# Gated DeltaNet stage of a decoder step: state scaling to GpSimd, first taps to ScalarE, masks by selection, z gates read from the PSUM bank

## The chip, the cores and the metric

The kernel runs on one NeuronCore of a Trainium2 chip. The metric is device time in microseconds for one call, the median of several runs. Five engines work side by side, each through its own instruction list in order: TensorE (PE, matmuls; PEld are its weight loads), VectorE (DVE), ScalarE (ACT), GpSimd (POOL) and SyncE (SP, which issues nearly all DMAs here). An instruction that waits holds up everything behind it on its engine.

## The reference, cut to what matters

One inference step of a decoder layer for 256 prompt tokens and 8 samples of 8 tokens each, 320 columns in all. One input projection feeds two branches: a gated DeltaNet (GDN) with 16 key heads and 32 value heads, and a sparse attention. The parts that the change touches:

```python
y = sum(xp[:, i:i + L] * w[i] for i in range(CONV_W)); silu(y)          # short convolution, 4 taps
decay = exp(where(incl, G[..., :, None] - G[..., None, :], -inf))        # causal mask on the gates
s = s * gt_c[..., None, None] + einsum('bhck,bhcv->bhkv', kt_c, u)       # matrix state, 128 x 128 per head and sample
y = rms_norm(o, gdn_norm_g) * silu(z)                                    # output norm, gated by z
```

## The kernel before, in words

All large projections are matmuls of 128 output channels by 320 columns. A weight block is streamed in two halves ("units") of 128 x 1024: SP loads it into `raw` (six halves in flight), ScalarE rounds it to `whi` (line 380), VectorE makes the remainder `wlo = raw - whi` (line 381), three buffers each, and TensorE does 24 matmuls per unit (`pm<-xh,whi`, `pm<-xl,whi`, `pm<-xh,wlo`, lines 403 to 410). This main stream runs from 205 us to the end; a unit is about 3.5 us of TensorE.

Everything else is side work: Python generators that emit a few instructions at a time between the units (`side_round`, line 305). What is emitted where is decided while the program is built, by a planner: the class `Clock` (lines 76 to 193) keeps a modelled time for each engine, a generator is resumed once the modelled TensorE time has reached the time that it last yielded, and `force` (line 329) emits side work at once when the main stream needs a buffer. So a price or a yield that is changed moves instructions on all engines, and on the chip each engine then runs its list in that fixed order.

The GDN stage lies at some 705 to 1660 us, in eight groups of two key heads (four value heads). For each group:

- `conv` (line 1761), 64 calls in the program: ScalarE copies a block to `xp`, VectorE does tap 0 as a TENSOR_SCALAR into a PSUM bank `u` and taps 1 to 3 as SCALAR_TENSOR_TENSOR, ScalarE the tanh (`cth`), VectorE the gate.
- `z_done` (line 1887), 28 calls, and `z_early` (line 1319), 4: ScalarE copies z with the norm's weight as scale, ScalarE does a tanh into a second tile, VectorE joins them, SP stores the result to DRAM (`d_z`). The tiles are the ring `zf` of four; `norm_gen` uses the same ring to load z again and store y (`d_ya`).
- `gb_gen` (line 1896), 16 calls: gates are loaded, VectorE adds a 128 x 384 mask `mask3` for two heads, ScalarE does six exponentials.
- `inverse` (line 2007), 8 calls: a 48 x 32 x 32 triangular inverse on GpSimd, 31 pairs of TENSOR_TENSOR (`tmpx`, `X`), then through DRAM (`d_x`): SP writes `X` and its transpose `blk`, reads 15 pieces back into `XT`, `X` and `blk`, and TensorE joins the blocks in four steps. All of this stands in SP's one queue together with the `raw` loads.
- `prompt_chain` and `sample_chain` (lines 2155 and 2232), 16 calls each: short matmuls with copies and scalings between them. At the end of `sample_chain` (lines 2279 to 2284) VectorE updates the state `S` (128 x 2048) with 16 SCALAR_TENSOR_TENSOR of 128 x 128, `S * gtr + ps`.
- `norm_gen` (line 2294), 16 calls: ScalarE squares `ot` six times into `sc`; VectorE, GpSimd (the power -0.5) and VectorE again make six factors; ScalarE scales `ot` with them, six instructions `ot<-ot,sc`, right behind whatever was emitted before.

In this trace every instruction shows the line of one helper (L64), so groups are told apart by tile names.

Of the kernel before, what the change touches and what calls it, by code (L numbers as in the profile page):

```python
# [17 lines left out]
NP = 256  # L18
# [57 lines left out]
class Clock:  # L76
# [54 lines left out]
    def cost(self, name, op, outs, ins):  # L131
        n = max(self.free(a) for a in outs[:1] + ins) if ins else self.free(outs[0])
        if name == "tensor":
            if op == "transpose":
                return 0.01 if ins[0].shape[0] == 32 else max(outs[0].shape[-1], 32) * 2 / 2400.0
            lhs, rhs = ins
            n = self.free(rhs)
            if lhs.dtype == F32R:
                return n * 1.1 / 2400.0
            if lhs.dtype == BF:  # L140
                return n / 2400.0
            k, m = lhs.shape[0], lhs.shape[1]
            part = 0.32 if m <= 32 else 0.62 if m <= 64 else 1.0
            part *= 0.29 if k == 32 and rhs.shape[1] == NB else 0.62 if k <= 64 else 1.0
            return max(n, 32) * 4 / 2400.0 * part + 0.01
        if name == "vector":
            fast = op in ("tensor_copy", "memset", "tensor_scalar")
            sb = all(a.space == outs[0].space for a in ins)
            return 0.16 + n * (0.0006 if fast and sb else 0.00106)
        if name == "scalar":  # L150
            return 0.19 + n * 0.00084 + 0.19 * (len(outs) > 1)
        if op == "memset":
            return 0.1 + n * 0.0009
        return 0.25 + n * (0.0018 if op == "tensor_copy" else 0.0028)
# [51 lines left out]
class Kernel:  # L206
# [1112 lines left out]
    def z_early(self, p, h):  # L1319
        self.force(lambda: len(self.t_r.free) >= 2)  # L1320
        z, t = self.t_r.get(), self.t_r.get()
        self.act(z, p[:, :NT], AF.Copy, scale=self.gh)
        self.act(t, p[:, :NT], AF.Tanh, scale=0.5)
        self.stt(z, t, 1.0, z, OP.add, OP.mult)
        self.t_r.put(t)
        self.store(self.d_z[h], z, self.t_r)
# [372 lines left out]
    def gdn_open(self):  # L1699
# [8 lines left out]
        self.mask3 = a.tile([128, 384], F32, name="mask3")  # L1708
# [19 lines left out]
        for c0, m0 in ((0, 0), (128, 0), (256, 128)):  # L1728
            nc.vector.tensor_copy(self.mask3[:, c0:c0 + 128], self.mask[:, m0:m0 + 128])
# [31 lines left out]
    def conv(self, p, cs, blk, dests, slot, then):  # L1761
# [11 lines left out]
        self.ts(u[:, 0:344], xp[:, 0:344], wv(0), None, OP.mult)  # L1773
# [113 lines left out]
    def z_done(self, p, h):  # L1887
        self.force(lambda: self.zf.free and self.cth.free)
        z, t = self.zf.get(), self.cth.get()
        self.act(z, p[:, :NT], AF.Copy, scale=self.gh)  # L1890
        self.act(t[:, :NT], p[:, :NT], AF.Tanh, scale=0.5)
        self.stt(z, t[:, :NT], 1.0, z, OP.add, OP.mult)
        self.cth.put(t)
        self.store(self.d_z[h], z, self.zf)

    def gb_gen(self, h):
# [7 lines left out]
        self.tt(gb, gb, self.mask3.rearrange("p (o i) -> p o i", o=1).to_broadcast([128, 2, 384]), OP.add)  # L1904
# [212 lines left out]
    @staticmethod  # L2117
    def scal(G, e):
        sst = G["sst"]
        s = lambda v, t: sst[:, 26 + 6 * e + 3 * v + t:27 + 6 * e + 3 * v + t]  # L2120
        stl = lambda v, t: sst[:, 38 + 6 * e + 3 * v + t:39 + 6 * e + 3 * v + t]
        return s, stl
# [32 lines left out]
    def prompt_chain(self, h, G):  # L2155
# [20 lines left out]
        for v in range(2):  # L2176
            self.ts(wt[:, v, :], p[:, 128 * v:128 * v + 128], stl(v, 0), None, OP.mult)
# [28 lines left out]
        for v in range(2):  # L2206
            self.ts(wt[:, v, :], p[:, 128 * v:128 * v + 128], stl(v, 1), None, OP.mult)
# [24 lines left out]
    def sample_chain(self, h, G):  # L2232
# [21 lines left out]
        self.R.put(R)  # L2254
        for v in range(2):
            self.stt(xr[:, v, :], p[:, 128 * v:128 * v + 128], self.neG[:, 2, hv + v:hv + v + 1], vt[:, 2, v, :],
                     OP.mult, OP.add)
# [11 lines left out]
        for v in range(2):  # L2269
            self.ts(wt[:, v, :], p[:, 128 * v:128 * v + 128], stl(v, 2), None, OP.mult)  # L2270
        self.ps_side.put(p)
        self.drop_T(G)
        yield
        yield from self.need(self.ps_side, 4)
# [19 lines left out]
    def norm_gen(self, h, G):  # L2294
# [294 lines left out]
```

## Time and profile before

| | |
|---|---|
| time, median of 3 runs | 2140.52 us (2138.27 to 2140.97) |
| profiled execution: its time, its span | 2134.91 us, 2133.2 us |
| TensorE busy | 2089.9 us, 98% |
| VectorE, ScalarE, GpSimd busy | 1419.2 us (67%), 968.4 us (45%), 464.1 us (22%) |
| mean share of the 16 DMA engines in use, in 50 us stretches of the GDN stage | 0.60 to 0.91 |

Rows of a waits view read: engine and tile, who ended the wait, total us, times, longest. Rows of a timeline: start, duration, engine, operation, tiles, and in brackets the idle time before it and who ended it. Rows of the grouped view: engine, operation, tiles, shape, count, busy us, mean ns of one, idle time before. Rows of a windows view: stretch and length, then busy us and count of PE, PEld, DVE, ACT and POOL, the granted TensorE clock, DMA share, GB/s.

### The profile page before, as it was taken

How to read it: one execution, taken by the hardware profiler on the slowest of the kernel's cores; microseconds unless marked ns; L12 is line 12 of the kernel's file. 1: busy time of each engine (PE TensorE's matmuls, PEld its weight loads, DVE VectorE, ACT ScalarE, POOL GpSimd, SP SyncE). 2: the span in 40 equal slices, each digit the busy share in tenths (PEclk: the TensorE clock that was granted, in tenths of full speed). 3: DMA queues.
4: the chain of work that ended last, by engine and by line, in shares of the span. 5: the costliest groups of instructions: out<-in, count | busy, mean ns of one | idle time of the engine just before them, and what ended most of it. 6: DMA issues, size and time to landing. Idle time of an engine off the chain costs nothing.

```text
span 2133.2 us, 45095 instructions
## 1 busy us (share of the span) xinstructions
PE 2089.9 (98%) x17741; PEld 2021.9 (95%) x17741; DVE 1419.2 (67%) x2858; ACT 968.4 (45%) x2202; POOL 464.1 (22%) x654
## 2 busy tenths in 40 slices
PE   7999999999999999989999999999999999999997
PEld 7999999999999999889999999999999999999997
DVE  4676658899845577857877787778665645445543
ACT  4225443333434455465646564656554534233343
POOL 1001000000010019441835082708080000000000
PEclk9999999999999999999999999999999999999999
DMA  9996658885696766766867686868687877555562
GB/s 346 333 337 183 189 155 258 242 256 146 190 282 191 222 174 177 192 179 180 229 176 209 173 231 166 221 169 244 163 242 213 250 208 212 167 155 146 166 179 83
DMA packets 714149, 439.04 MB, mean 206 GB/s; under 512 B 73968, under 2 KB 697296, under 8 KB 711632
## 3 DMA queue, kind: packets, MB, share of 16 engines
q1 hardware_dynamic: 709856, 413.50, 68.8%
q0 software_dynamic: 3616, 21.02, 2.8%
q8 instruction: 139, 2.28, 0.4%
q10 hardware_dynamic: 464, 1.65, 0.2%
q14 instruction: 74, 0.61, 0.1%
HBM read 386.81 MB, written 48.94 MB: 204 GB/s over the span
## 4 chain that ended last, share of the span: by engine, by line
PE 64%; issue 22%; DVE 5%; ACT 3%; DMA 3%; SPq 1%; POOL 1%; DVEq 0%; POOLq 0%; ACTq 0%
PE pm L64 49%; PE ps L64 14%; DVE S L64 2%; SPq L64 1%; DVE wlo L64 1%; DMA raw<-in_w_ada_dram 1%; ACT whi L64 1%; DVE ps L64 1%; ACT ot L64 1%; ACT ps L64 1%; DMA rawx<-in_w_ada_dram 1%; POOL X L64 0%; ACT vt L64 0%; POOL tmpx L64 0%; DVE w L64 0%
## 5 line engine op out<-in xcount | busy, mean ns | idle before, releaser
L64 PE MATMUL pm<-xh,whi 128*128 128x320 f32 (+1 forms) x3108 | 941.3, 317 | 10.4 <-ACT whi L64 9.1
L64 PE MATMUL pm<-xl,whi 128*128 128x320 f32 (+1 forms) x3108 | 911.8, 307 | 0.4 <-DVE xl L64 0.3
L64 DVE TENSOR_TENSOR wlo<-raw,whi 128x1024 fp32r<-128x1024 f32 x466 | 586.7, 1267 | 258.7 <-ACT whi L64 242.2
L64 PEld LDWEIGHTS pm<-xh,whi 128*128 128x128 f32 x3108 | 586.0, 189 | 33.6 <-issue 17.6
L64 PEld LDWEIGHTS pm<-xl,whi 128*128 128x128 f32 x3108 | 586.4, 189 | 1.5 <-DVE xl L64 0.8
L64 ACT ACTIVATE whi<-raw 128x1024 fp32r<-128x1024 f32 x466 | 489.7, 1059 | 176.7 <-PE pm L64 109.4
L64 PE MATMUL pm<-xh,wlo 128*128 128x320 f32 (+1 forms) x3108 | 522.7, 308 | 2.5 <-DVE wlo L64 2.4
L64 PEld LDWEIGHTS pm<-xh,wlo 128*128 128x128 f32 x3108 | 470.2, 188 | 3.8 <-DVE wlo L64 3.7
L64 POOL TENSOR_TENSOR X<-X,tmpx 48x31 f32<-48x31 f32 (+15 forms) x248 | 182.1, 734 | 19.4
L64 POOL TENSOR_TENSOR tmpx<-blk,X 48x31 f32<-48x31 f32 (+15 forms) x248 | 162.8, 656 | 105.6 <-DMA blk<-d_b 87.6
L64 DVE SCALAR_TENSOR_TENSOR ps<-xp,cs,ps 128x344 f32<-128x344 f32 x192 | 111.5, 581 | 6.8
L64 POOL TENSOR_TENSOR sc<-sc,mh 128x6 f32<-128x6 f32 (+1 forms) x24 | 41.7, 1736 | 297.9 <-DVE sc L64 261.4
L64 PE MATMUL pm<-y1h,whi 128*128 128x320 f32 x336 | 99.5, 309 | 1.3 <-ACT whi L64 0.9
L64 POOL TENSOR_TENSOR rfin<-rfin,mh 128x3 f32<-128x3 f32 x1 | 0.8, 848 | 455.0 <-DVE rfin L64 455.0
L64 PE MATMUL pm<-y1l,whi 128*128 128x320 f32 x336 | 99.2, 308 | 0.0
L64 ACT ACTIVATE xp<-pm 128x256 f32<-128x256 f32 (+1 forms) x128 | 31.9, 302 | 83.4 <-PE pm L64 83.4
L64 POOL DMA_INDIRECT a<-in_cache_k_dram,idx x8 | 7.5, 936 | 280.2 <-PE ps L64 265.3
L64 DVE SCALAR_TENSOR_TENSOR S<-S,gtr,ps 128x128 f32<-128x128 f32 x256 | 67.4, 341 | 0.3 <-PE ps L64 0.3
L64 PE MATMUL ps<-xh,whi 128*128 128x320 f32 (+1 forms) x220 | 64.7, 309 | 0.0
L64 PEld LDWEIGHTS pm<-y1h,whi 128*128 128x128 f32 x336 | 62.9, 187 | 1.8 <-ACT whi L64 1.8
L64 PE MATMUL ps<-xl,whi 128*128 128x320 f32 (+1 forms) x220 | 63.7, 304 | 0.0
L64 PEld LDWEIGHTS pm<-y1l,whi 128*128 128x128 f32 x336 | 63.0, 187 | 0.0
(415 smaller groups left out, 2774.5 us busy)
## 6 DMA issues: line engine op xcount, KB each, us to landing
raw<-in_w_in_dram SPq DMA_DIRECT2D x328, 512.0 KB
raw<-in_w_pa_dram SPq DMA_DIRECT2D x64, 512.0 KB
rawx<-in_w_ada_dram SPq DMA_DIRECT2D x18, 1024.0 KB
a<-in_w_ada_dram SPq DMA_DIRECT2D x16, 1024.0 KB
S<-in_state_gdn_dram SPq DMA_DIRECT2D x32, 512.0 KB
out_dram<-S SPq DMA_DIRECT2D x32, 512.0 KB
raw<-in_w_pb_dram SPq DMA_DIRECT2D x32, 512.0 KB
raw<-in_w_out_dram SPq DMA_DIRECT2D x32, 512.0 KB
```

The lines of the kernel that those rows point to most:

```text
L64: made = fn(*args, **kw)
```

## The change

- State: GpSimd scales `S` by the decay in one TENSOR_TENSOR of 128 x 2048 as soon as the matmuls that read the old state are emitted; VectorE then only adds, four TENSOR_TENSOR of 128 x 512, one per bank.
- Convolution: tap 0 goes to ScalarE (a Copy with scale, from `xp` into the bank).
- Masks: `mask3` is gone; GpSimd writes the mask value by five AFFINE_SELECT per head pair. The planner gets a price for that operation.
- z: one tanh into the tile, and VectorE reads the other factor from the PSUM bank; the norm's weight moves into the last product of `norm_gen`. The second tile is no longer needed.
- The two scalings of `wt` per step become one TENSOR_TENSOR over both heads.
- `norm_gen`: one VectorE instruction fewer, the EPS added by GpSimd, and a new yield 1.5 us of modelled time behind the factors before the six ScalarE scalings are emitted. `sample_chain` yields until `S` is scaled before the last matmuls are emitted.

```diff
             return 0.19 + n * 0.00084 + 0.19 * (len(outs) > 1)
-        if op == "memset":
-            return 0.1 + n * 0.0009
+        if op in ("memset", "affine_select"):
+            return (0.1 if op == "memset" else 0.3) + n * 0.0009
         return 0.25 + n * (0.0018 if op == "tensor_copy" else 0.0028)
...
-        self.mask3 = a.tile([128, 384], F32, name="mask3")
...
         wv = lambda t: cs[:, blk, 24 + t:25 + t]
-        self.ts(u[:, 0:344], xp[:, 0:344], wv(0), None, OP.mult)
+        self.act(u[:, 0:344], xp[:, 0:344], AF.Copy, scale=wv(0))
         for t in range(1, 4):
...
     def z_done(self, p, h):
-        self.force(lambda: self.zf.free and self.cth.free)
-        z, t = self.zf.get(), self.cth.get()
-        self.act(z, p[:, :NT], AF.Copy, scale=self.gh)
-        self.act(t[:, :NT], p[:, :NT], AF.Tanh, scale=0.5)
-        self.stt(z, t[:, :NT], 1.0, z, OP.add, OP.mult)
-        self.cth.put(t)
+        self.force(lambda: self.zf.free)
+        z = self.zf.get()
+        self.act(z, p[:, :NT], AF.Tanh, scale=0.5)
+        self.stt(z, z, 1.0, p[:, :NT], OP.add, OP.mult)
         self.store(self.d_z[h], z, self.zf)
...
         yield
-        self.tt(gb, gb, self.mask3.rearrange("p (o i) -> p o i", o=1).to_broadcast([128, 2, 384]), OP.add)
+        self.emitted += 1
+        g = gb[:, :, 0:256].rearrange("p v (t i) -> p v t i", t=2)
+        nc.gpsimd.affine_select(g, g, pattern=[[0, 2], [0, 2], [1, 128]], compare_op=OP.is_ge, fill=NEG, base=0,
+                                channel_multiplier=-1)
+        for v in range(2):
+            g = gb[:, v, 256:384].rearrange("p (b q) -> p b q", b=8)
+            nc.gpsimd.affine_select(g, g, pattern=[[-16, 8], [0, 16]], compare_op=OP.is_ge, fill=NEG, base=0,
+                                    channel_multiplier=1)
+            g = gb[:, v, 256:384].rearrange("p (b q t) -> p b q t", b=8, q=2)
+            nc.gpsimd.affine_select(g, g, pattern=[[16, 8], [0, 2], [1, 8]], compare_op=OP.is_ge, fill=NEG, base=0,
+                                    channel_multiplier=-1)
         yield
...
         s = lambda v, t: sst[:, 26 + 6 * e + 3 * v + t:27 + 6 * e + 3 * v + t]
-        stl = lambda v, t: sst[:, 38 + 6 * e + 3 * v + t:39 + 6 * e + 3 * v + t]
+        stl = lambda t: sst[:, 38 + 6 * e + t:38 + 6 * e + 4 + t:3].rearrange("p (v o) -> p v o", o=1).to_broadcast([128, 2, 128])
         return s, stl
...
             self.act(wf[:, v, :], p[:, 128 * v:128 * v + 128], AF.Copy, scale=s(v, 0))
-        for v in range(2):
-            self.ts(wt[:, v, :], p[:, 128 * v:128 * v + 128], stl(v, 0), None, OP.mult)
+        self.tt(wt, p[:, 0:256].rearrange("p (v d) -> p v d", v=2), stl(0), OP.mult)
         self.ps_side.put(p)
...
             self.act(x1[:, v, :], p[:, 128 * v:128 * v + 128], AF.Copy, scale=s(v, 1))
-        for v in range(2):
-            self.ts(wt[:, v, :], p[:, 128 * v:128 * v + 128], stl(v, 1), None, OP.mult)
+        self.tt(wt, p[:, 0:256].rearrange("p (v d) -> p v d", v=2), stl(1), OP.mult)
         self.ps_side.put(p)
...
         self.R.put(R)
+        self.tt(S, S, self.gtr[:, :, hv:hv + 2].rearrange("p b (v o) -> p b v o", o=1).to_broadcast([128, NB, 2, 128]),
+                OP.mult, eng=nc.gpsimd)
         for v in range(2):
...
         self.act(ot[:, 2], p[:, 0:256].rearrange("p (v d) -> p v d", v=2))
-        for v in range(2):
-            self.ts(wt[:, v, :], p[:, 128 * v:128 * v + 128], stl(v, 2), None, OP.mult)
+        self.tt(wt, p[:, 0:256].rearrange("p (v d) -> p v d", v=2), stl(2), OP.mult)
         self.ps_side.put(p)
         yield
+        yield self.ready(S)
         yield from self.need(self.ps_side, 4)
         for j in range(4):
-            for pp in range(2):
-                for v in range(2):
-                    bb = 2 * j + pp
-                    self.stt(S[:, bb, v, :], S[:, bb, v, :], self.gtr[:, bb, hv + v:hv + v + 1],
-                             ps[j][:, 256 * pp + 128 * v:256 * pp + 128 * v + 128], OP.mult, OP.add)
+            sj = S[:, 2 * j:2 * j + 2].rearrange("p b v d -> p (b v d)")
+            self.tt(sj, ps[j], sj, OP.add)
             self.ps_side.put(ps[j])
...
         self.tt(mv(6), mv(0), qf, OP.mult)
-        self.tt(mv(6), mv(6), qf, OP.mult)
-        self.ts(m[:, 6:12], m[:, 6:12], 1.0 / 128, EPS, OP.mult, OP.add)
+        self.stt(mv(6), mv(6), 1.0 / 128, qf, OP.mult, OP.mult)
+        self.ts(m[:, 6:12], m[:, 6:12], EPS, None, OP.add, eng=nc.gpsimd)
         self.tt(m[:, 12:18], m[:, 6:12], self.mh.to_broadcast([128, 6]), OP.pow, eng=nc.gpsimd)
         self.tt(mv(12), mv(12), qf, OP.mult)
+        yield self.ready(m) + 1.5
         for t in range(3):
...
             z = y = zs[v]
-            self.tt(y[:, 0:NP], p[:, 0:NP], z[:, 0:NP], OP.mult)
-            self.tt(y[:, NP:NT].rearrange("p (b t) -> p b t", t=TS),
-                    p[:, NP:384].rearrange("p (b q t) -> p b q t", q=2, t=TS)[:, :, 1, :],
-                    z[:, NP:NT].rearrange("p (b t) -> p b t", t=TS), OP.mult)
+            self.stt(y[:, 0:NP], p[:, 0:NP], self.gh, z[:, 0:NP], OP.mult, OP.mult)
+            self.stt(y[:, NP:NT].rearrange("p (b t) -> p b t", t=TS),
+                     p[:, NP:384].rearrange("p (b q t) -> p b q t", q=2, t=TS)[:, :, 1, :], self.gh,
+                     z[:, NP:NT].rearrange("p (b t) -> p b t", t=TS), OP.mult, OP.mult)
             self.ps_side.put(p)
```

(`z_early` is changed as `z_done` is, with the ring `t_r`.)

What the change moves, at three places. Names: `whi`, `wlo`, `raw` are the weight halves; `ot` a head's output, `sc` its factors; `cth`, `xp`, `ps_68` belong to a convolution; `S` is the state.

Place 1, the norm of the third group's first head, ScalarE before:

```order
L64 ACTIVATE vt_7856<-ps_70,sc_7871 128x128 x2
L64 ACTIVATE ps_72,sc_7868<-ot_7864 128x128 x6
L64 ACTIVATE whi_80<-raw_75 128x1024
L64 ACTIVATE xp_7819<-pm_65 128x256
L64 ACTIVATE xp_7819<-pm_65 128x8x8
L64 ACTIVATE xp_7819<-cs_102 128x8x3
L64 ACTIVATE ot_7864<-ot_7864,sc_7868 128x128 x6
L64 ACTIVATE whi_78<-raw_76 128x1024
L64 ACTIVATE whi_79<-raw_76 128x1024
```

and now (its tiles are `ot_7859`, `sc_7865`):

```order
L64 ACTIVATE whi_80<-raw_77 128x1024
L64 ACTIVATE vt_7851<-ps_72,sc_7863 128x256 x2
L64 ACTIVATE vt_7851<-ps_70,sc_7863 128x256
L64 ACTIVATE whi_78<-raw_77 128x1024
L64 ACTIVATE cth_7816<-ps_68 128x344
L64 ACTIVATE xp_7815<-pm_65 128x256
L64 ACTIVATE xp_7815<-pm_65 128x8x8
L64 ACTIVATE xp_7815<-cs_101 128x8x3
L64 ACTIVATE ps_68<-xp_7815,cs_101 128x344
L64 ACTIVATE ot_7859<-ot_7859,sc_7865 128x128 x6
L64 ACTIVATE ps_67,sc_7865<-ot_7860 128x128 x6
L64 ACTIVATE whi_79<-raw_75 128x1024
```

Between the squares (`ps,sc<-ot`) and the six scalings (`ot<-ot,sc`) stood one conversion to `whi`; now four stand there, two of them in the rows shown, and the squares are nine instructions ahead of these rows. Tap 0 of a convolution (`ps_68<-xp`) is new in the list.

The same place on VectorE, which makes the last factor (`sc<-sc,sc`, 128x6, once), before:

```order
L64 SCALAR_TENSOR_TENSOR S_7867<-S_7867,gtr,ps_69 128x128 x4
L64 SCALAR_TENSOR_TENSOR S_7867<-S_7867,gtr,ps_67 128x128 x4
L64 SCALAR_TENSOR_TENSOR S_7867<-S_7867,gtr,ps_70 128x128 x4
L64 SCALAR_TENSOR_TENSOR S_7867<-S_7867,gtr,ps_72 128x128 x4
L64 COPY ct_7823<-xp_7819 128x27
L64 TENSOR_SCALAR ps_68<-xp_7819,cs_102 128x344
L64 SCALAR_TENSOR_TENSOR ps_68<-xp_7819,cs_102,ps_68 128x344 x3
L64 TENSOR_TENSOR sc_7868<-sc_7868,sc_7871 128x6
L64 TENSOR_TENSOR wlo_81<-raw_76,whi_78 128x1024
L64 TENSOR_TENSOR wlo_82<-raw_76,whi_79 128x1024
```

and now:

```order
L64 TENSOR_TENSOR wlo_81<-raw_76,whi_78 128x1024
L64 TENSOR_TENSOR S_7862<-ps_72,S_7862 128x512
L64 TENSOR_TENSOR S_7862<-ps_70,S_7862 128x512
L64 TENSOR_TENSOR S_7862<-ps_67,S_7862 128x512
L64 TENSOR_TENSOR S_7862<-ps_69,S_7862 128x512
L64 SCALAR_TENSOR_TENSOR vf_7831<-cth_7816,ps_68 128x256
L64 SCALAR_TENSOR_TENSOR vf_7831<-cth_7816,ps_68 128x8x8
L64 TENSOR_TENSOR wlo_82<-raw_76,whi_79 128x1024
L64 COPY ct_7817<-xp_7814 128x27
L64 SCALAR_TENSOR_TENSOR ps_68<-xp_7814,cs_101,ps_68 128x344 x3
L64 TENSOR_TENSOR sc_7865<-sc_7865,sc_7866 128x6
L64 TENSOR_TENSOR wlo_83<-raw_77,whi_80 128x1024
```

The factor stood behind 16 state updates, tap 0 and taps 1 to 3, and ahead of the `wlo` that belong to the two `whi` that ScalarE makes behind its scalings; now four additions and no tap 0 stand ahead of it, and it stands ahead of the `wlo` of two `whi` (`raw_77`; one is the last row) that ScalarE makes before its scalings.

Place 2, SP's queue around the second group's inverse, before (`d_x` is the inverse's way through DRAM, `zf` the z and y tiles, `d_b` and `d_o` the next group's matrix; eleven reads back are cut by the line of dots):

```order
L64 DMA raw_76<-in_w_in_dram 128x8x128 x2
L64 DMA d_ya<-zf_7839 128x320
L64 DMA d_x_95<-X 48x1024
L64 DMA d_x_95<-blk 48x1024
L64 DMA blk<-d_o_97 64x4x64 x2
L64 DMA blk<-d_o_97 32x8x32 x2
L64 DMA XT_7852<-d_x_95 32x12x32
...
L64 DMA X<-d_x_95 32x4x32
L64 DMA raw_77<-in_w_in_dram 128x8x128
L64 DMA d_ya<-zf_7841 128x320
L64 DMA raw_77<-in_w_in_dram 128x8x128
```

and now:

```order
L64 DMA d_ya<-zf_7837 128x320
L64 DMA d_x_95<-X 48x1024
L64 DMA d_x_95<-blk 48x1024
L64 DMA raw_77<-in_w_in_dram 128x8x128
L64 DMA blk<-d_o_97 64x4x64 x2
L64 DMA blk<-d_o_97 32x8x32 x2
L64 DMA XT_7847<-d_x_95 32x12x32
...
L64 DMA X<-d_x_95 32x4x32
L64 DMA d_b_92<-BT_7840 32x12x32 x4
L64 DMA d_o_96<-BT_7840 512x1x64
L64 DMA d_o_96<-BT_7840 256x1x32 x2
L64 DMA raw_77<-in_w_in_dram 128x8x128
```

One `raw` load has moved in between the inverse's writes and its reads, the second and later y stores (`d_ya`) ahead of the writes, and seven writes of the next group's matrix behind the reads, ahead of the next `raw`.

Place 3, GpSimd at the end of the same inverse and the start of the next, before:

```order
L64 TENSOR_TENSOR X<-X,tmpx 48x31
L64 COPY blk<-X 48x1024
L64 MEMSET X 32x8x32
L64 MEMSET X 32x4x32 x2
L64 TENSOR_TENSOR sc_7871<-sc_7871,mh 128x10
L64 TENSOR_TENSOR sc_7870<-sc_7870,mh 128x6
L64 MEMSET X 48x1024
L64 MEMSET X 48x32
```

and now:

```order
L64 TENSOR_TENSOR X<-X,tmpx 48x31
L64 COPY blk<-X 48x1024
L64 MEMSET X 32x8x32
L64 MEMSET X 32x4x32 x2
L64 TENSOR_TENSOR S_7861<-S_7861,gtr 128x2048
L64 TENSOR_TENSOR S_7862<-S_7862,gtr 128x2048
L64 MEMSET X 48x1024
L64 MEMSET X 48x32
```

Two state scalings stand between the end of one inverse and the start of the next.

More of the change, by code (lines that the diff above doesn't have):

```diff
@@ L1319, in z_early @@
     def z_early(self, p, h):
-        self.force(lambda: len(self.t_r.free) >= 2)
-        z, t = self.t_r.get(), self.t_r.get()
-        self.act(z, p[:, :NT], AF.Copy, scale=self.gh)
-        self.act(t, p[:, :NT], AF.Tanh, scale=0.5)
-        self.stt(z, t, 1.0, z, OP.add, OP.mult)
-        self.t_r.put(t)
+        self.force(lambda: self.t_r.free)
+        z = self.t_r.get()
+        self.act(z, p[:, :NT], AF.Tanh, scale=0.5)
+        self.stt(z, z, 1.0, p[:, :NT], OP.add, OP.mult)
         self.store(self.d_z[h], z, self.t_r)
@@ L1727, in gdn_open @@
         self.sc = Ring([b.tile([128, 56], F32, name=f"sc{j}") for j in range(4)])
-        for c0, m0 in ((0, 0), (128, 0), (256, 128)):
-            nc.vector.tensor_copy(self.mask3[:, c0:c0 + 128], self.mask[:, m0:m0 + 128])
         for r in (self.xp.free, ):
@@ L1887, in z_done @@
     def z_done(self, p, h):
-        self.force(lambda: self.zf.free and self.cth.free)
-        z, t = self.zf.get(), self.cth.get()
-        self.act(z, p[:, :NT], AF.Copy, scale=self.gh)
-        self.act(t[:, :NT], p[:, :NT], AF.Tanh, scale=0.5)
-        self.stt(z, t[:, :NT], 1.0, z, OP.add, OP.mult)
-        self.cth.put(t)
+        self.force(lambda: self.zf.free)
+        z = self.zf.get()
+        self.act(z, p[:, :NT], AF.Tanh, scale=0.5)
+        self.stt(z, z, 1.0, p[:, :NT], OP.add, OP.mult)
         self.store(self.d_z[h], z, self.zf)
```

## The prediction

> **What bounds the kernel now.** I read the page first, then stretches of 50 us, then the waits of TensorE in the GDN stage, then the timelines at its longest waits.
>
> ```profile
> span 2133.2 us, 45095 instructions
> PE 2089.9 (98%) x17741; PEld 2021.9 (95%) x17741; DVE 1419.2 (67%) x2858; ACT 968.4 (45%) x2202; POOL 464.1 (22%) x654
> ```
>
> TensorE is busy for all but 43.3 us, and the change leaves its instructions as they are. So the time can fall by no more than waits in the stretch that the change reaches, and rise by what new waits there are.
>
> ```profile
> 950.00:1000.00 50.00, 45.59 (x397) 42.10 (x398) 32.68 (x92) 26.16 (x75) 4.32 (x4) 0.93 0.60 166
> ```
>
> In this stretch, the worst of the GDN stage, TensorE loses 4.4 us and 7% of its clock. The waits of TensorE from 850 to 1700 us, longest in total first:
>
> ```profile
> PE pm L64 <- ACT whi L64: 10.0, 7, 4.4
> PE ps L64 <- DMA cst<-in_conv_w_dram: 2.1, 2, 1.9
> PE pm L64 <- DVE wlo L64: 1.9, 2, 1.7
> PE ps L64 <- DVE S L64: 1.2, 3, 0.6
> PE ps L64 <- DVE w L64: 1.1, 1, 1.1
> ```
>
> These are 16.3 us: late weight halves 11.9 us, of which one wait is 4.4 us. Why are they late? ScalarE's own largest wait on VectorE in this stage:
>
> ```profile
> ACT ot L64 <- DVE sc L64: 66.5, 16, 6.1
> ```
>
> All 16 norms hold ScalarE, 4.2 us each on average, in front of its six scalings, and the next `whi` queues behind them. ScalarE at one of them, then VectorE there:
>
> ```profile
> 1125.54 1.87 ACT L64 ACTIVATE ot<-ot,sc 128x128 f32<-128x128 f32 x6 [5.23 <-DVE sc L64]
> 1127.31 1.99 ACT L64 ACTIVATE whi<-raw 128x1024 fp32r<-128x1024 f32 x2
> ```
>
> ```profile
> 1118.46 4.21 DVE L64 SCALAR_TENSOR_TENSOR S<-S,gtr,ps 128x128 f32<-128x128 f32 x16
> 1122.60 0.17 DVE L64 COPY ct<-xp 128x27 f32<-128x27 f32 x1
> 1122.69 0.57 DVE L64 TENSOR_SCALAR ps<-xp,cs 128x344 f32<-128x344 f32 x1
> 1123.30 1.81 DVE L64 SCALAR_TENSOR_TENSOR ps<-xp,cs,ps 128x344 f32<-128x344 f32 x3
> 1125.02 0.48 DVE L64 TENSOR_TENSOR sc<-sc,sc 128x6 f32<-128x6 f32 x1
> ```
>
> The factor (last row) waits for nothing but its turn: 16 state updates and a convolution are ahead. TensorE then waits for the `whi` of 1127.31. The 4.4 us wait, which ends at 956.34, has another cause, shown by ScalarE and SP's queue:
>
> ```profile
> 951.83 0.53 ACT L64 ACTIVATE zf<-pm,gh 128x320 f32<-128x320 f32 x1 [9.17 <-issue]
> ```
>
> ```profile
> 930.20 1.66 SPq L64 DMA_DIRECT2D raw<-in_w_in_dram  x2
> ...
> 946.80 0.39 SPq L64 DMA_DIRECT2D raw<-in_w_in_dram  x1
> 947.29 0.52 SPq L64 DMA_DIRECT2D d_ya<-zf  x1
> ```
>
> ScalarE stood 9.17 us before a z copy. I take it that it waited for a z tile whose y store was issued only at 947.29, behind the inverse's writes and 15 reads, which also hold `raw` from 931.9 to 946.8; the trace names no releaser. After this wait, and after 1365 us, the clock is down:
>
> ```profile
> 951.00:957.00 6.00, 1.59 (x9) 1.33 (x8) 1.34 (x3) 5.05 (x17) 1.30 (x1) 0.75 0.74 225
> 957.00:963.00 6.00, 6.00 (x81) 5.76 (x81) 3.41 (x4) 2.96 (x7) 0.65 (x1) 0.68 0.93 265
> ...
> 1365.00:1372.00 7.00, 4.38 (x24) 4.14 (x25) 5.66 (x11) 5.59 (x14) 6.29 (x10) 0.88 1.12 304
> 1372.00:1385.00 13.00, 13.00 (x89) 12.98 (x87) 11.28 (x24) 7.78 (x26) 9.42 (x15) 0.93 0.61 160
> ```
>
> The first costs about 0.32 x 6 + 0.25 x 1 = 2.2 us, the second 0.12 x 7 + 0.07 x 13 = 1.7 us. The Trainium skill (TensorE: Matmul & The Clock Gate, Part 1) lets the clock fall to half after an idle window of about 3.4 us. The first pair agrees; in the second TensorE idled 2.6 us of 7, in two pieces, and the clock fell all the same, so I count by the rows; by the rule alone the 1.7 us would not have been lost.
>
> **The change part by part.** Prices on VectorE and ScalarE in the stage:
>
> ```profile
> L64 DVE TENSOR_TENSOR wlo<-raw,whi 128x1024 fp32r<-128x1024 f32 x210 | 276.3, 1323 | 83.1 <-ACT whi L64 76.0 <-PE pm L64 5.0 <-DMA raw<-in_w_in_dram 1.1
> ...
> L64 DVE SCALAR_TENSOR_TENSOR S<-S,gtr,ps 128x128 f32<-128x128 f32 x256 | 67.4, 341 | 0.3 <-PE ps L64 0.3
> L64 DVE TENSOR_SCALAR ps<-xp,cs 128x344 f32<-128x344 f32 x60 | 34.6, 577 | 0.4
> L64 DVE TENSOR_SCALAR w<-ps,sc 128x128 f32<-128x128 f32 x96 | 28.5, 344 | 19.5 <-ACT ot L64 16.6 <-ACT vt L64 2.8
> ...
> L64 DVE TENSOR_TENSOR gbt<-gbt,mask 128x768 f32<-128x768 f32 x14 | 16.8, 1202 | 0.0
> ...
> L64 DVE TENSOR_TENSOR PT<-ps,gbt 128x256 f32<-128x256 f32 x32 | 11.9, 414 | 0.6 <-PE ps L64 0.6
> ```
>
> ```profile
> L64 ACT ACTIVATE ot<-ot,sc 128x128 f32<-128x128 f32 x96 | 29.9, 390 | 66.5 <-DVE sc L64 66.5
> L64 ACT ACTIVATE cth<-ps 128x344 f32<-128x344 f32 x60 | 27.2, 454 | 40.8 <-DVE ps L64 40.7
> ...
> L64 ACT ACTIVATE zf<-pm,gh 128x320 f32<-128x320 f32 x28 | 14.8, 527 | 45.6 <-PE pm L64 36.4 <-issue 9.2
> ```
>
> *VectorE* loses tap 0 (64 x 0.577 = 37 us), the masks (16 x 1.2 = 19 us) and, of the states, 67.4 us against 64 additions of 128x512: between 0.414 us for 256 columns and 1.323 for 1024 a straight line gives 0.72, 46 us, so 21 saved. The 96 scalings `w` (28.5 us) become 48 products at 0.414, 20 us: 9 saved. Together 86 us less, with 4.21 us falling to some 2.9 at every state. VectorE is on TensorE's path only through late `wlo` and the norm's factor, so this is no term of its own.
>
> *ScalarE* gains 64 first taps, a form that the trace lacks: at least the 0.454 of the tanh over as many columns, at most 0.577, as VectorE took; I take 0.5, 32 us. It loses 32 copies of z, 17 us. The 15 us lie beside waits such as the 66.5 us; without that cover each tap makes a `whi` 0.5 us later.
>
> *GpSimd*'s rows:
>
> ```profile
> L64 POOL COPY blk<-X 48x1024 f32<-48x1024 f32 x8 | 16.6, 2069 | 0.5
> L64 POOL TENSOR_TENSOR X<-X,tmpx 48x255 f32<-48x255 f32 x16 | 15.9, 992 | 1.3
> ...
> L64 POOL TENSOR_TENSOR tmpx<-blk,X 48x31 f32<-48x31 f32 x16 | 5.6, 349 | 88.2 <-DMA blk<-d_b 87.6
> ...
> L64 POOL TENSOR_SCALAR_AFFINE_SELECT esel<-esel 32x512 bf16<-32x512 bf16 x4 | 5.2, 1305 | 0.3
> ...
> L64 POOL TENSOR_SCALAR_AFFINE_SELECT mask<-mask 128x128 f32<-128x128 f32 x3 | 1.1, 374 | 0.8 <-DVE mask L64 0.8
> ```
>
> A state scaling of 2048 columns costs at least two copies of 1024 (4.1 us) and at most the slope of the products, (0.992 - 0.349) / 224 = 2.9 ns a column, 6.2 us; it has two inputs as they have, so I take 5.5, 88 us for 16. Five selects: 4 x 0.374 and one over 512 between 0.4 and 1.3: 2.4 us, 38 us for 16. The EPS, as a small product, 0.35 us: 6 us. So 132 us more on GpSimd, some 16 us in a group of 107 us (855 us over eight). That can be hidden; in the queue it lies, by the third place shown above, between one inverse and the next, and with the selects inside an inverse, which becomes longer by some 5 us. [...]
>
> Does more GpSimd slow VectorE? From 1700 to 2100 us GpSimd does nothing, and there a `wlo` takes 1222 ns instead of 1323:
>
> ```profile
> L64 DVE TENSOR_TENSOR wlo<-raw,whi 128x1024 fp32r<-128x1024 f32 x113 | 136.8, 1222 | 73.4 <-ACT whi L64 71.8 <-PE pm L64 1.0 <-PE ps L64 0.5
> ```
>
> If all 0.1 us is GpSimd's doing, 132 us more on its 464 make the average `wlo` 0.03 us longer, against 3.5 us of TensorE for a unit: no term. The Trainium skill (GPSIMD Engine Reference, 1. Specifications) has GpSimd and VectorE share their SBUF interfaces when a VectorE instruction reads two SBUF inputs, as `wlo` does; the rows agree.
>
> *The terms on TensorE's path*, against the profiled execution (span 2133.2, time 2134.9; the median of the runs is 5.6 us higher):
>
> A. The norm. By the first place, four conversions instead of one lie between squares and scalings, and the factor stands ahead of two `wlo` more, each 1.3 us. So ScalarE's wait goes nearly everywhere. Late halves other than the 4.4 us are 11.9 - 4.4 = 7.5 us; not all follow a norm: **-6**.
>
> B. The z tile. By the second place the y stores now stand ahead of the inverse's writes. 4.4 + 2.2 = 6.6 us is at stake, but seven more writes stand ahead of the next `raw`, which in this trace came 15 us after its predecessor: **-5**.
>
> C. The wait for `cst` at 1369.65 (1.9 us) with the clock after it (1.7): it follows a norm wait of 1.3 us, and I take two thirds: **-2.5**.
>
> D. `force`: at the third group's start the program has to finish the first group's chains at once (877 to 894 us; the waits for `S` and `w`, 2.3 us, are there). Additions are shorter, but two steps of the inverse now fall into that stretch: **+1**.
>
> E. New waits: VectorE's additions hold every `wlo` behind them until GpSimd has scaled, and six norm squares may queue behind it. At least nothing, at most as much as all late halves now, 7.5: **+2**.
>
> Sum -10.5: span 2122.7, its time 2124.4, and a median of 2130.
>
> **Rivals.**
>
> R1, all of it goes: 16.3 us of waits and 3.9 of clock, 2120. For it: VectorE's load falls by a seventh in this stage. Against: the list is new, and the same planner left these waits.
>
> R2, the waits move: A is real, but others of the same sort take their place, since `whi` is only some us ahead and ScalarE has 15 us more: -10.5 + 8 = -2.5, 2138.
>
> R3, slower: GpSimd ends its inverse late. SP stands at `d_x<-X` with all `raw` behind it, as it does by up to 5.1 us now:
>
> ```profile
> SPq L64 <- POOL X L64: 13.5, 8, 5.1
> ```
>
> If the added 5 us come on top of that, an inverse holds `raw` for 20 us instead of 15; from there each costs what the one at 956 did, 6.6 us. Four of eight: 26.4, less A and C: some +18, 2158; two of eight: +5, 2145.
>
> R4, the hold does not do what it says: if VectorE drifts more than 1.5 us behind the model, the scalings still wait: -10.5 + 6 = -4.5, 2136.
>
> **How the numbers follow.** Forecast 0.43, R1 0.12, R2 0.22, R3 0.13, R4 0.10. What a measurement can tell from no change is 0.2%, 4.3 us: faster is below 2136.2, slower above 2144.8. Faster: 0.41 + 0.12 + 0.05 + 0.05 = 0.63. Slower: 0.11 + 0.03 + 0.01 = 0.15. Same: 0.22. The range runs from R1 to the border of slower, 2120 to 2144.
>
> **What would show it.** A: the row of ScalarE's wait on `sc` falls from 66.5 to under 20 us, TensorE's wait for `whi` from 10.0 to about 3. B and C: no granted clock under 0.95 between 850 and 1700 us. Prices: state scaling 4.1 to 6.2 us, tap 0 on ScalarE 0.45 to 0.58. D: 877 to 894 us no longer than 19. R3: SP's wait on POOL's `X` above 30 us. I am wrong if TensorE's waits in the stage stay above 13 us with the time down, or if the time moves outside these stretches, where the list hardly changes.

## The result and the profile after

The changed kernel takes 2115.12 us (median of 4 runs, 2112.19 to 2118.39) against 2139.85 us (4 runs, 2138.27 to 2140.97): a ratio of 0.9885, 95% interval 0.9868 to 0.9902. It is faster by 24.7 us, where 10 were forecast and 20 were the most that I counted as possible from the profile. The profiled executions, 2114.43 and 2134.91 us, differ by 20.5 us. One execution, of the kernel with the hold and tap 0 below, took 5248.55 us where the other four took 2130.70 to 2131.94 us; it is left out of every ratio.

The page of the changed kernel:

```profile
span 2112.7 us, 44968 instructions
PE 2081.9 (99%) x17741; PEld 2019.2 (96%) x17741; DVE 1352.8 (64%) x2519; ACT 991.2 (47%) x2234; POOL 563.7 (27%) x766
```

TensorE's idle time falls from 43.3 to 30.8 us, its busy time by 8.0 us with the same instructions. The fall in idle time lies in the GDN stage. The view by windows, the kernel before first, then the changed one (stretch, length, busy us of PE, PEld, DVE, ACT, POOL, clock, DMA share, GB/s):

```profile
850.00:1700.00 850.00, 832.36 (x6761) 794.83 (x6761) 621.08 (x1451) 468.85 (x1263) 363.14 (x502) 0.99 0.75 201
```

```profile
850.00:1700.00 850.00, 845.47 (x6900) 812.29 (x6900) 577.72 (x1141) 498.09 (x1306) 452.12 (x594) 1.00 0.77 207
```

17.6 us of idle TensorE became 4.5, and the clock is full. What is left, by the waits of the changed kernel in that stretch:

```profile
PE ps L64 <- DMA cst<-in_conv_w_dram: 3.1, 3, 1.2
PE ps L64 <- DVE S L64: 0.5, 1, 0.5
PE ps L64 <- ACT XT L64: 0.5, 1, 0.5
```

No late weight half is among them: 11.9 us have become nothing. ScalarE's groups, of the norm's scalings and of the new first tap, show why:

```profile
L64 ACT ACTIVATE ps<-xp,cs 128x344 f32<-128x344 f32 x60 | 33.1, 552 | 8.2 <-DVE ct L64 3.4 <-DVE vf L64 1.8 <-DVE R L64 1.4
L64 ACT ACTIVATE ot<-ot,sc 128x128 f32<-128x128 f32 x96 | 29.6, 388 | 0.0
```

The scalings stood 66.5 us behind the factor; now 0.0. The new prices on VectorE and GpSimd (stretch 760 to 1700 us, as for the rows before):

```profile
L64 DVE TENSOR_TENSOR wlo<-raw,whi 128x1024 fp32r<-128x1024 f32 x215 | 292.8, 1364 | 88.8 <-ACT whi L64 75.4 <-PE pm L64 10.5 <-DMA raw<-in_w_in_dram 1.3
...
L64 DVE TENSOR_TENSOR S<-ps,S 128x512 f32<-128x512 f32 x64 | 39.7, 682 | 2.6 <-PE ps L64 2.0 <-POOL tmpx L64 0.5
```

```profile
L64 POOL TENSOR_TENSOR S<-S,gtr 128x2048 f32<-128x2048 f32 x16 | 60.8, 3807 | 158.8 <-DMA raw<-in_w_in_dram 76.3 <-issue 74.1 <-PE ps L64 8.4
L64 POOL TENSOR_SCALAR_AFFINE_SELECT gbt<-gbt 128x128 f32<-128x128 f32 x56 | 27.2, 497 | 1.9
```

A state scaling takes 3.8 us, below the bound of 4.1 that I drew from copies; a select 0.50 instead of 0.37; a bank's addition 0.68 (0.72 forecast); tap 0 on ScalarE 0.55 (0.5). VectorE is 66 us lighter (86 forecast), GpSimd 100 us heavier (132), ScalarE 23 us heavier (15).

### The profile page after: what moved, and what is told of

It is laid out like the page before. It is cut to its first block, busy times and chain, and to the rows that moved or that the text cites. A ratio compares the mean times of both kernels' runs of the same rounds, so it can differ in the third digit from the quotient of the medians.

```text
span 2112.7 us, 44968 instructions
## 1 busy us (share of the span) xinstructions
PE 2081.9 (99%) x17741; PEld 2019.2 (96%) x17741; DVE 1352.8 (64%) x2519; ACT 991.2 (47%) x2234; POOL 563.7 (27%) x766
## 4 chain that ended last, share of the span: by engine, by line
PE 70%; issue 23%; DMA 3%; SPq 1%; DVE 1%; ACT 1%; POOL 0%; DVEq 0%; POOLq 0%; ACTq 0%
PE pm L64 55%; PE ps L64 15%; SPq L64 1%; DMA cst<-in_conv_w_dram 1%; DMA raw<-in_w_in_dram 1%; DMA rawx<-in_w_ada_dram 1%; DMA raw<-in_w_ada_dram 0%; DVE wlo L64 0%; DMA out_dram<-sall 0%; POOL sc L64 0%; POOL S L64 0%; ACT whi L64 0%; DVE sga L64 0%; DVEq L2586 0%; DVE scp L64 0%
## 5 line engine op out<-in xcount | busy, mean ns | idle before, releaser
L64 DVE TENSOR_TENSOR wlo<-raw,whi 128x1024 fp32r<-128x1024 f32 x466 | 597.2, 1287 | 266.3 <-ACT whi L64 239.6
L64 POOL TENSOR_TENSOR tmpx<-blk,X 48x31 f32<-48x31 f32 (+15 forms) x248 | 157.3, 634 | 44.5 <-DMA blk<-d_b 27.8
L64 POOL TENSOR_TENSOR S<-S,gtr 128x2048 f32<-128x2048 f32 x16 | 60.8, 3807 | 158.8 <-DMA raw<-in_w_in_dram 76.3
L64 ACT ACTIVATE vt<-ps,sc 128x128 f32<-128x128 f32 (+1 forms) x112 | 39.1, 412 | 58.2 <-PE ps L64 58.1
```

The costliest lines, as they stand in the source:

```text
L64: made = fn(*args, **kw)
```

## The experiments

There are three theories. **W**: ScalarE's wait for the norm's factor is the cause, and the new hold (the yield of 1.5 us ahead of the six scalings) takes it away. **L**: the lighter VectorE is the cause. **F**: the time is set by how often the planner has to emit side work at once because a buffer is asked for before it is free (`force`), and the hold works through the order of the lists. I had `force` count, while the program is built, the units of the GDN stage at which it found a buffer taken. (The first expectations say H for the theory of the hold, before it was split into W and F, and N for a third: any new list would lose the long stall and the half clock.) The table has every run's main numbers (idle TensorE is 850 us less its busy time in the stretch 850 to 1700 us; waits are of the same stretch; all us):

| kernel | forced units | scalings wait on `sc` | TensorE waits for `whi` | idle TensorE | ratio of times, 95% interval |
|---|---|---|---|---|---|
| before | 26 | 66.5 | 10.0 | 17.6 | 1 |
| changed | 10 | 0.0 | 0 | 4.5 | 0.9885 (0.9868 to 0.9902) |
| before + hold | 6 | 0.0 | 0 | 3.1 | 0.9892 (0.9878 to 0.9906) |
| before + hold of zero | 6 | 1.9 | 0 | 3.1 | 0.9888 (0.9870 to 0.9905) |
| changed, masks on VectorE | 4 | 0.0 | 0 | 0.0 | 0.9879 (0.9862 to 0.9896) |
| changed, state on VectorE | 5 | 0.0 | 0 | 7.4 | 0.9951 (0.9938 to 0.9963) |
| before + hold + tap 0 on ScalarE | 18 | 0.2 | 7.1 | 12.9 | 0.9962 (0.9946 to 0.9978) |
| changed without hold | 21 | 46.3 | 6.8 | 13.0 | 0.9983 (0.9974 to 0.9992) |
| before + z part | 21 | 68.7 | 4.4 | 14.9 | 0.9985 (0.9975 to 0.9994) |
| before + state part | 25 | 70.2 | 3.4 | 20.9 | 1.0055 (1.0042 to 1.0068) |
| before, no wait on `sc`, same lists | 26 | 0.0 | 4.9 | 11.3 | 0.9958 (0.9945 to 0.9971) |
| before, y store by GpSimd, same lists | 26 | 66.5 | 9.9 | 17.5 | 1.0008 (0.9999 to 1.0017) |
| both of these, same lists | 26 | 0.0 | 5.0 | 11.3 | 0.9950 (0.9938 to 0.9961) |
| changed + a second GpSimd pass, same lists | 10 | 2.2 | 1.6 | 15.1 | 0.9983 (0.9974 to 0.9992) |

(The expectations say 5 for the hold alone; counted by units it is 6. For the state part the waits for `cst`, not for `whi`, are the large ones.)

**1. The hold taken out, and the hold alone.**

```diff
-        yield self.ready(m) + 1.5          # changed kernel without the hold
+        yield self.ready(m) + 1.5          # kernel before, with nothing but the hold
```

> The changed kernel without the new yield of 1.5 us in front of the six ScalarE scalings of the norm (its list has 1 to 3 conversions to whi between squares and scalings instead of 3 to 5). Theory H (the hold is the cause): ScalarE's wait on sc comes back, from 0 to over 40 us, and with it late weight halves of 5 us or more; time 2121 to 2127. Rival L (VectorE's and GpSimd's shorter or moved work is the cause, the hold does little): the factor comes earlier by itself, wait on sc under 25 us, time within 3 us of the changed kernel, 2113 to 2118.

> The kernel before with nothing but the new yield of 1.5 us in front of the norm's scalings (3 to 5 conversions between squares and scalings). Theory H: ScalarE's wait on sc falls from 66.5 to under 15 us, TensorE's late halves behind norms go (some 7 us), the stall of 4.4 us at 956 us may stay: 2126 to 2133. Rival L: 2136 to 2140. A third, N (any new list loses the two stretches of half clock and the stall at 956 us, whatever the edit): 2129 to 2134 here and in every other variant of the kernel before.

Without the hold all other parts together give 0.9983, some 4 us, and the wait is back at 46.3 us, as H said; the time, 2131.7 us, lies above all the ranges. The hold alone gives 0.9892, as much as the whole change and more than any range allowed. L is out as the cause. The kernel with the hold alone has no wait of TensorE for a weight half any more; its waits are those of the forced stretch:

```profile
PE ps L64 <- DVE S L64: 1.2, 3, 0.6
PE ps L64 <- DVE w L64: 1.1, 1, 1.1
PE ps L64 <- DVE vt L64: 0.4, 1, 0.4
```

Its 23 us are more than the 7.5 us of late halves that I took to follow norms, and more than the 13.5 us of my terms A, B and C.

**2. The state part alone, and the change without it.** The diff is that of the change at the end of `sample_chain`, put in alone, and taken out (with it the yield for the scaled state).

> The kernel before with only the state part: GpSimd scales S, VectorE adds a bank at a time, the last matmuls yield until S is scaled. Theory H: the norm keeps 1 or 2 conversions between squares and scalings, so late halves stay: 2135 to 2142. Rival L: the state was the longest piece of VectorE's work ahead of the factor (4.2 us, now 2.7), so most of the gain is here: 2122 to 2130. N: 2129 to 2134.

> The changed kernel with the state update back on VectorE as it was (16 instructions of 128x128, nothing on GpSimd). Theory H: the hold still works, 2 to 5 conversions in between: within 4 us of the changed kernel, 2113 to 2120. Rival L: 2124 to 2132. If GpSimd's scaling itself costs something, this is below 2113.

All three theories (H, L and N) missed the first: it is slower by 12 us. With the last matmuls held for the scaled state, the chains of every group are now emitted at one go: TensorE has stretches of 14.5 us with 114 side matmuls and no main stream, near 988, 1101, 1214, 1329 and 1442 us, besides the one near 880 us that all these kernels have. Some 34 us behind the end of each of the five it waits, 1.8 to 3.6 us, and then runs at about half clock (waits of TensorE, then two of the windows):

```profile
PE ps L64 <- DMA cst<-in_state_conv_dram: 5.9, 2, 3.6
PE ps L64 <- DMA cst<-in_conv_w_dram: 4.0, 2, 2.2
PE pm L64 <- ACT whi L64: 3.4, 2, 1.8
PE ps L64 <- DVE w L64: 3.1, 6, 0.6
```

```profile
1036.00:1040.00 4.00, 4.00 (x19) 4.00 (x19) 3.93 (x5) 4.00 (x12) 3.69 (x5) 0.57 0.92 264
...
1490.00:1494.00 4.00, 3.96 (x16) 3.96 (x17) 3.89 (x6) 4.00 (x12) 3.69 (x5) 0.57 0.92 261
```

That the long stretches cause these waits is argued from the constant distance; no run shows it. The count of forced units does not tell the two kernels apart, 25 against 26.

The second, 2126.3 us, lies in L's range and outside H's, although the hold alone rules L out. It has few forced units, but its one forced stretch is long: 24.2 us with 146 side matmuls, against 15.8 us with 106 in the kernel before. TensorE's clock falls in it, it waits there for VectorE's `w`, and once more at 911 us, for `vf`:

```profile
PE ps L64 <- DVE vf L64: 3.4, 1, 3.4
PE ps L64 <- DVE w L64: 1.8, 1, 1.8
```

```profile
892.00:899.00 7.00, 5.19 (x20) 4.54 (x20) 4.50 (x17) 1.25 (x4) 6.22 (x11) 0.50 0.72 207
```

So the same part is worth -14 us with the hold and the rest (0.9885 against 0.9951), and +12 us alone. Its own work cannot be what decides, since that is the same in both.

**3. The hold without its margin; the hold with another edit that brings the forced units back.**

```diff
+        yield self.ready(m) + 0.0          # before, hold of zero
```

```diff
+        yield self.ready(m) + 1.5          # before, hold and tap 0
-        self.ts(u[:, 0:344], xp[:, 0:344], wv(0), None, OP.mult)
+        self.act(u[:, 0:344], xp[:, 0:344], AF.Copy, scale=wv(0))
```

> The kernel before with a yield in front of the norm's scalings that waits only until the factor is ready by the planner's clock, without the 1.5 us on top (2 to 4 conversions between squares and scalings, where the 1.5 us give 3 to 5). If the margin against drift is what counts (my case R4): ScalarE's wait on sc 10 to 35 us, 2120 to 2128. If it counts that the planner may go on with other work at all: wait on sc under 8 us, 2113 to 2119.

> The kernel before with the hold of 1.5 us and tap 0 of the convolutions on ScalarE. The norm has 3 to 5 conversions between squares and scalings as with the hold alone, but while the program is built 18 buffers in the stage are asked for before they are free (calls of force that have to emit side work at once), where the hold alone has 5 and the kernel before 26. Theory W (the wait on sc alone sets the time): 2113 to 2118. Theory F (the forced emissions set it, and the hold works by leaving few of them): wait on sc near 0 and yet 2124 to 2134.

The margin of 1.5 us does not matter: without it 1.9 us of wait are left, and the time is the same. My case R4 has no ground. The second lies in F's range: no wait on the factor, and yet 0.9962, with 7.1 us of late `whi`. ScalarE now stands elsewhere in front of its `whi`. One such place is the first taps of convolutions (its waits, then one of them in its timeline):

```profile
ACT ps L64 <- DVE ct L64: 37.2, 18, 5.3
```

```profile
1150.81 0.55 ACT L64 ACTIVATE ps<-xp,cs 128x344 f32<-128x344 f32 x1 [5.26 <-DVE ct L64]
1151.30 1.04 ACT L64 ACTIVATE whi<-raw 128x1024 fp32r<-128x1024 f32 x1
```

The longest of TensorE's late halves here, 2.66 us up to 1500.61 us, has another: a z copy that waits for the store of its tile. SyncE issues that store right behind the reads of an inverse (SyncE, then ScalarE):

```profile
1496.18 0.47 SPq L64 DMA_DIRECT2D X<-d_x  x1
1496.75 0.38 SPq L64 DMA_DIRECT2D d_z<-zf  x1
```

```profile
1498.76 0.53 ACT L64 ACTIVATE zf<-pm,gh 128x320 f32<-128x320 f32 x1 [5.50 <-DMA d_z<-zf]
1499.50 2.00 ACT L64 ACTIVATE whi<-raw 128x1024 fp32r<-128x1024 f32 x2
```

This is the mechanism of term B, with a z store in place of a y store and the releaser named. W as I had put it is too narrow. What makes `whi` late is any instruction that is put into ScalarE's list before its operand can be there; the norm's scalings were the largest of these, not the only ones.

**4. The z part alone, and the masks back on VectorE.** Both diffs are pieces of the change.

> The kernel before with only the z part (one tanh into the tile, VectorE reads the other factor from the bank, the norm's weight in the last product); no hold, 1 to 3 conversions between squares and scalings, 21 forced buffers in the stage. Theory W: the wait on sc stays at 50 to 70 us and the time at 2133 to 2141. Theory F: 21 against 26 is little, 2129 to 2138. My term B (the stall at 956 us is the z tile's, and goes when its y store is queued elsewhere): no wait of TensorE over 3 us, 2130 to 2134.

> The changed kernel with the masks added by VectorE as before (no selects on GpSimd). 4 forced buffers in the stage where the changed kernel has 10. Theory F: 2109 to 2115. Theory W (no wait on sc is left to win, 16 additions of 1.2 us come back to VectorE): 2114 to 2120.

The z part gives 0.9985: with 21 forced units it keeps the wait of 68.7 us and has no wait over 2.4 us. Its time lies in the ranges of W and of F alike, so it does not separate them. For B the waits fit and the time is too slow by 2 us; it does not settle B, since its lists differ from those of the kernel before at the place of that stall. The masks on VectorE give a stage without a single wait of TensorE:

```profile
850.00:1700.00 850.00, 850.00 (x6941) 818.50 (x6940) 599.15 (x1165) 498.36 (x1308) 431.33 (x535) 1.00 0.77 209
```

Its time, 2113.92 us and 0.9879, cannot be told from the changed kernel's or the hold's. The selects on GpSimd bring nothing that can be measured, and little more is to be had in this stage.

**5. The same lists, one cause taken away.** These two edits hide from the planner what they change, so that every engine's list stays as it was, but for the store that the second edit moves. In the first, the six scalings read a constant and wait for nothing (it leaves out the norm's factor, so y is scaled wrongly; all work is done). In the second, one store of y is issued by GpSimd, which has nothing to do then.

```diff
-                self.act(ot[:, t, v, :], ot[:, t, v, :], AF.Copy, scale=m[:, 12 + 2 * t + v:13 + 2 * t + v])
+                nc.scalar.engine.activation(ot[:, t, v, :], ot[:, t, v, :], AF.Copy, scale=self.gh)
+                nc.scalar.enter(...)               # the planner books the old operands
```

```diff
+            if hv + v == 1:
+                nc.gpsimd.engine.dma_start(self.d_ya[hv + v], y)
+                nc.gpsimd.enter(...)               # booked as SyncE's
```

> The kernel before with every engine's list as it is, and one thing changed: the norm's six scalings on ScalarE read a constant that has long been there instead of the factor, so they wait for nothing (y is scaled wrongly, all work is done; the planner is told of the old operand, so no instruction moves). Theory A (my term: the wait itself makes late weight halves, worth 6 us, and the second half-clock stretch 2.5): ScalarE's wait on sc 0, 2129 to 2134. Theory F (the hold works through the order of the lists, the wait is a sign of it): 2134 to 2139. Theory W (the wait on sc alone sets the time): 2113 to 2120.

> The kernel before with every list as it is but for one instruction: the y store of the second head, the one issued at 947 us behind the inverse's reads, is issued by GpSimd instead of SyncE. Term B (ScalarE's z copy at 951 us waits for that store, and TensorE's stall of 4.4 us and the half clock behind it come from it): the z copy starts by 946 us, no stall over 2 us at 956, 2131 to 2135. If the stall came from raw, which is held for the same 15 us: the stall stays above 3 us, 2137 to 2141.

> Both edits at once on the old lists: no wait on sc, and the one y store by GpSimd. If A, B and C of the prediction are the right places and sizes, this has their sum, 13.5 us: 2124 to 2128. If the rest of the changed kernel's gain lies in other places of the list, it stays above 2129; if the two account for all of it, 2113 to 2119.

Without the wait, 0.9958: 9.0 us (6.2 to 11.7). On the old lists the wait itself is worth that and no more, some 40% of what the hold gives. The time, 2127.0 us, lies in none of the three ranges: the wait is worth more than A's terms, and far less than W needs. TensorE's waits for the halves are all gone but one, and the one for `cst` is there and longer:

```profile
PE pm L64 <- ACT whi L64: 4.9, 1, 4.9
PE ps L64 <- DMA cst<-in_conv_w_dram: 3.2, 1, 3.2
PE ps L64 <- DVE S L64: 1.2, 3, 0.6
```

Behind each of these two the clock falls as before: it is 0.77 from 955 to 961 us and 0.76 from 1364 to 1371 us. The two waits and their clock are 4.9 + 1.4 + 3.2 + 1.7 = 11.2 us, most of the 14 us by which the hold gains more than this run.

The run of the y store does not test term B, because it moved another store. The second head's (`hv + v == 1`) is the one that SyncE issued at 949.21 us in the kernel before. The one issued at 947.29 us is that of `zf_7841` in the queue shown under place 2, the third head's, and SyncE still issues it behind the inverse's reads. GpSimd, SyncE and ScalarE in this run:

```profile
940.28 0.68 POOL L2346 DMA_DIRECT2D d_ya<-zf  x1 [1.95 <-DVE zf L64]
```

```profile
947.39 0.39 SPq L64 DMA_DIRECT2D raw<-in_w_in_dram  x1
947.88 0.52 SPq L64 DMA_DIRECT2D d_ya<-zf  x1
```

```profile
952.38 0.53 ACT L64 ACTIVATE zf<-pm,gh 128x320 f32<-128x320 f32 x1 [9.15 <-issue]
955.80 1.99 ACT L64 ACTIVATE whi<-raw 128x1024 fp32r<-128x1024 f32 x2
```

In the built program this z copy writes `zf_7841`, and it waits for that tile's y store and for the matmuls of its own block. The block had ended on TensorE at 943.5 us in the kernel before, 8 us ahead of the copy (the `wlo` row at 942.20, followed by the transposes that the program has behind that block):

```profile
942.20 1.34 PE L64 MATMUL pm<-xh,wlo 128*128 128x320 f32 x8
943.38 0.38 PE L64 MATMUL ps<-ident,kq 128*128 128x128 f32 x2
```

So the store is what it waited for. The copy starts 4.5 to 4.7 us after the issue of that store in all four kernels with these lists (947.29 and 951.83, 947.88 and 952.38, 945.32 and 949.91, 948.79 and 953.50 us). With both edits the view puts the same wait down to TensorE:

```profile
953.50 0.53 ACT L64 ACTIVATE zf<-pm,gh 128x320 f32<-128x320 f32 x1 [9.68 <-PE pm L64]
956.92 1.99 ACT L64 ACTIVATE whi<-raw 128x1024 fp32r<-128x1024 f32 x2
```

That releaser is inferred, and it fits only the end of the next block, which the copy does not read and which in the first two of these kernels ends 0.1 us after the copy's start. The kernel with both edits is thus the one without the wait once more: 0.9950 against 0.9958. That its time, 2126.3 us, lies in the range of A, B and C together is luck, for the stall of B is there, 5.0 us long.

Behind the copy the list has the squares of the keys and only then the next `whi`, 3.4 us after the copy's start and without a gap; so `raw`, held by SyncE for the same time, is not what `whi` waited for. The wait is written into two lists: the store behind the inverse's reads on SyncE, and the `whi` behind the copy and the squares on ScalarE. In the kernel with the hold alone the second y store (944.65 us) stands ahead of the reads, z copies wait 1.7 and 0.7 us for such stores, and TensorE waits for no `whi`. What this stall costs by itself was not measured: no run took away that one wait.

So the 14 us come from the order of the lists. F as I had put it, with the count of forced units as what sets the time, is not shown: the kernel with five (state on VectorE) is slower than the changed kernel with ten, and 25 or 26 give anything from 0.9950 to 1.0055. The count goes with the time in most rows of the table; no run changes it alone.

**6. More work for GpSimd on the same lists.**

```diff
         self.tt(S, S, self.gtr[...], OP.mult, eng=nc.gpsimd)
+        nc.gpsimd.engine.tensor_scalar(S, S, 1.0, None, op0=OP.mult)   # the planner is not told
```

> The changed kernel with a second pass of GpSimd over each state (a product with 1.0 over 128x2048, 2 to 4 us, 16 times) that the planner is not told of, so every list stays as it is. Rival R3 of the prediction (GpSimd's inverse late, SyncE held at the write of X) says when that begins: if GpSimd has slack in every group, 2114 to 2117; if 2 to 4 us in front of an inverse are too much, SyncE's wait on POOL's X rises from 2.8 to over 20 us and the time to 2120 or more.

The pass took 5.9 us rather than 2 to 4, and nearly the whole gain is gone: 0.9983 against 0.9885. GpSimd, SyncE's wait on it, and TensorE:

```profile
L2258 POOL TENSOR_SCALAR S<-S 128x2048 f32<-128x2048 f32 x16 | 93.7, 5856 | 1.4
```

```profile
SPq L64 <- POOL X L64: 20.4, 8, 7.9
```

```profile
PE ps L64 <- DMA X<-d_x: 5.4, 2, 3.0
PE ps L64 <- DVE w L64: 3.8, 4, 1.9
PE pm L64 <- ACT whi L64: 1.6, 2, 1.3
```

GpSimd is busy for 66% of the stage here and 53% in the changed kernel, and it still sits on the path: the two scalings of a group lie directly ahead of the next inverse, and already the second inverse began 11 us later than in the changed kernel (896.1 against 885.4 us), the seventh 16 us (1427.2 against 1411.4). Two passes are 11.7 us; the changed kernel has less slack than that in a group. R3 is a real mechanism, which this change does not reach and 11.7 us more in each group do.

## Why the prediction was wrong, by its steps

The direction and the first place were right: all late halves are gone, and with them ScalarE's 66.5 us. The size was half of what came. By the terms, with what the profiles and runs show:

- **A, the norm, -6.** The 7.5 us of late halves besides the one at 956 us are all gone, and gone without a rearranged list too. The wait itself was worth 9.0 us (6.2 to 11.7). My discount ("not all follow a norm") was wrong.
- **B, -5.** The mechanism was right: the z copy waited for the tile whose y store stood behind the inverse's reads. The stall of 4.4 us and the half clock behind it went, some 6.6 us; the discount, for seven more writes ahead of the next `raw`, was not needed.
- **C, -2.5.** The half clock there went (1.7 us), the wait for `cst` did not: 2.1 us became 3.1, in three pieces of which none lowered the clock. It does not come from the norm: with the norm's wait away it is 3.2 us, and the clock falls behind it all the same. What brings `cst` late stays open.
- **D, +1.** The wrong sign. The forced stretch lost 2.9 us of TensorE before and loses 1.0 now, though two steps of the inverse fall into it.
- **E, +2.** No such cost is in the changed kernel. TensorE's waits for `S` and `w` are 0.8 us there and were 2.3 before, and VectorE's additions waited 2.6 us in all, 0.5 of them for GpSimd.

In the profiled executions idle TensorE accounts for 12.5 us and the lost clock for 3.9, 16.4 us where the sum had 10.5; some 4 us of the fall in TensorE's busy time I can give to no row. The other 4.2 us of the 24.7 are my step from the profile to the median: the kernel before lies 4.9 us above its profiled execution (5.6 by the three runs that I had), I let the changed kernel lie as far above its own, and it lies 0.7 above. This step is nearly all of what put the time below my range: R1's 20.2 us were close to the 20.5 of the profiles, but its time of 2120 carried the 5.6 us.

The step that failed is the sizing of the sum: A and B were set below what the rows had at stake, 7.5 and 6.6 us, and D and E added 3 us of new costs that no run shows. R1, "all of it goes", was nearest to what came, and I gave it 0.12, with the argument that the same planner had left these waits.

Nor did I see that one yield does nearly all of it. The hold changes what the planner books: ScalarE no longer stands in its books behind the factor, convolutions find their buffers free, and 6 units are forced instead of 26. Taking the wait away on the old lists gives 9 us, the hold 23; most of the 14 us between them are two places that the lists themselves had made, the stall at 956 us with its clock and the wait for `cst` with its clock.

I also took the lighter VectorE for a help. Without the hold all that is worth 4 us, and with the hold nothing that can be measured: the hold alone, one line, is as fast as the whole change. Single parts are not neutral, though: taking the state part out of the changed kernel costs 14 us.

What stays open: why the state part brings a long stretch of side work in every group when it stands alone, and only the first one when it stands with the rest. TensorE's timelines say that it does; which of the planner's bookings tips it was not tried.

## What to carry to other kernels

Where a program is laid out by a planner, ask of each wait whether the engine is slow or the instruction was put into an in-order list too early: the first is cured by faster work, the second by not emitting the instruction until its operand is due, which costs one line. Take a wait away on unchanged lists (another operand, the planner told of the old one) before you credit an edit that also moves everything else, and see in the trace that the instruction you meant is the one that moved: of two stores 2 us apart, the y store's run moved the wrong one. Where the view names no releaser, or one of several, look up in the program which tile the instruction writes. Slack of an engine is what it has ahead of its next piece on the path, not the idle share of its busy row.

## What the runs showed of the hardware

- The clock fell to about half after single waits of TensorE of 1.8, 2.2, 2.3, 2.4 and 2.7 us: it was 0.57 to 0.60 in the 4 us behind each. It stayed at 1.00 after waits of 1.9 us (the second GpSimd pass, 1103 us), 2.6 us (the changed kernel without the hold, 1032 us) and 3.4 us (state on VectorE, 911 us). The Trainium skill (TensorE: Matmul & The Clock Gate, Part 1) ties it to an idle window of about 3.4 us that runs freely. The waits that lowered the clock here are all shorter, so here the measurement decides: a wait of 2 us may cost nearly as much again in clock (0.43 of 4 us), or nothing.
- On GpSimd a TENSOR_SCALAR over 128x2048 fp32 takes 5.9 us, a TENSOR_TENSOR with a broadcast operand of the same size 3.8 us. Here one input less is not cheaper.
- `wlo` takes 1222 ns with GpSimd idle, 1323 ns with it busy for 43% of the stage, 1364 ns with 53% and 1442 ns with 66%.
